# Hybrid decoder block on one core: first four row tiles transposed by TensorE, other buffer counts, sub-norm factors folded into the output weights

## The chip, the cores and the metric

The kernel runs on one core of one Trainium2 chip. The metric is the device time of one execution in microseconds, the median of several runs. The engines are TensorE (PE; PEld is its weight load), VectorE (DVE), ScalarE (ACT), GpSimd (POOL) and SyncE (SP), which issues nearly all DMAs.

## The reference

One layer on x of 2048 tokens by 1024 features, f32:

```
h    = RMSNorm(x)
cq, ckv, kr, dq, dk, dv, mq, z = split(h @ w_in)      # D_IN = 2464
A    = latent attention, 8 heads: causal softmax(q k^T / sqrt(96)) v, q and k normed, 32 of 96 columns rotated
B    = differential attention, 4 heads: (softmax_1 - lambda softmax_2) v, then
       rms_norm(o, diff_subln_g) * (1 - lam_init)      # the sub-norm, per head of 64 columns
C    = cross attention of the tokens into 256 memory tokens (4 heads), memory normed and projected first
out  = x + (concat(A, B, C) * silu(z)) @ w_out         # 512 + 256 + 256 columns
```

## The kernel before, in words

Tokens lie in 16 row tiles of 128, and four of these make a block (b = 0 to 3). Every f32 operand of a projection is split into a high and a low f16 half, and a product is three matmuls, high by high, high by low, low by high (`project`, lines 173 to 178).

`normed_t` (lines 129 to 140) takes one row tile: ScalarE squares and sums it (L132), GpSimd makes the reciprocal root (`rstd_of`, L97 and L101), ScalarE writes the scaled tile rounded to f16, the high half (L134), VectorE writes the remainder, the low half (L138). Both halves need features on the partitions, so SP issues one DMA transpose for each (L136, L139) into `ht`, 128 x 2 x 8 x 128. These DMA instructions are collected in the list `turned`. `load` (lines 116 to 122), which fetches rows and weights, looks at this list: as long as it has between 1 and 11 entries, the load is issued under `tc.issue_after` an entry some places back (3 or 6). That adds an order, without a semaphore, behind the named instruction for those instructions of the block that are on its engine. So SP issues the early loads behind transposes.

`m_prep` for block 0 (lines 1049 to 1074) fetches rows 0 to 3 and the first weights and norms the four tiles; then `x_feed` does the other twelve tiles, and `mem_kv` norms the memory's two tiles in the same way and projects them. `rope_tables` (lines 252 to 289) makes the rotary tables from the positions, in two scratch tiles of the tag `t4`, which has two buffers.

The work goes in 28 steps: 4 of C ("m"), 8 of B ("d", two head pairs by four blocks), 16 of A ("a", four head pairs by four blocks). A step has a preparation (projection, norms, rotation, transposes, estimate of the row maximum) and a main part.

- The estimate is `est_block` (lines 374 to 408). It computes the scores of high halves alone. For blocks 1 to 3 ScalarE copies the first score tile of a row tile into `er` as bf16 (L391), each further one into `ec` (L394), and VectorE takes the larger of `er` and `ec` (L395). Two row tiles share one `er`; after both, VectorE halves it three times (L399) and reduces it (L400). There are 96 such pairs in the kernel. `er` has two buffers, `ec` three. The maximum goes into the query operand as a further row, so the main scores come out shifted by it.
- The main part is `Map` (lines 475 to 524). `head` computes a score tile on TensorE (`st`), ScalarE writes its exponential as f32 into `p32` (L493; the profile calls this tile p), VectorE writes the low part into `plo` (L494). `tail` multiplies the upper 16 bits of `p32` (L503, L505) and `plo` (L523) with the values. `p32` has three buffers, `plo` four, the score tile two of PSUM.
- After a d step `post_d` (lines 577 to 594) applies the sub-norm: squares on ScalarE, the reciprocal root on GpSimd, then three VectorE passes over 128 x 512: by the root (L588), by the gain `g_sub` that holds (1 - lam_init) / 64 (L589), by the gate (L592).

`load_wout` (lines 920 to 929) fetches the output weights in chunks of 128 rows and splits them, scaled by WS = 64; chunks 4 and 5 are those of B. `out_tile` divides by it again with a factor 0.5 / WS.

What sets the order: preparations, main units and fills (`fills`, lines 1146 to 1160: memory, further rows, gates, latents, output projection) are generators. A loop (lines 1189 to 1225) advances the one with the least due time, worked out from costs written by hand. That gives the order in which instructions are traced, and with offsets a priority. From these a scheduler, which keeps a simulated time line, writes each engine's fixed order. A tile with n buffers makes the writer of use i wait for the readers of use i - n.

Of the kernel before, what the change touches and what calls it, by code (L numbers as in the profile page):

```python
# [11 lines left out]
F32 = mybir.dt.float32  # L12
F16 = mybir.dt.float16
BF16 = mybir.dt.bfloat16
# [5 lines left out]
P = 128  # L20
# [20 lines left out]
def hybrid_block(ctx: ExitStack, tc: tile.TileContext, x, mem, positions, norm_g, w_in, mla_q_norm_g,  # L41
# [84 lines left out]
        load(xt, src, pace)  # L126
        return xt

    def normed_t(xt, name):
        hi = stack([P, DM], f"xh_{name}")  # L130
        ss = sm.tile([P, 1], F32, tag="ss1", name=f"ss_{name}")
        A.activation(hi, xt, AF.Square, scale=1.0 / math.sqrt(DM), accum_out=ss)  # L132
        r = rstd_of(ss, [1], f"r_{name}", "rstd_x")
        A.activation(hi, xt, AF.Copy, scale=r)  # L134
        ht = bigt([P, 2, NK, P], f"ht_{name}")
        turned.append(SP.dma_start_transpose(ht[:, 0], hi))  # L136
        lo = stack([P, DM], f"xl_{name}")
        V.scalar_tensor_tensor(lo, xt, r, hi, ALU.mult, ALU.subtract)  # L138
        turned.append(SP.dma_start_transpose(ht[:, 1], lo))  # L139
        return ht  # L140


# [48 lines left out]
    def tmp4(name):  # L191
        return wk.tile([P, 1024], F32, tag="t4", name=name, bufs=2)
# [57 lines left out]
    sin_t = cst.tile([P, NT, 16], F32, name="sin_t")  # L250

    def rope_tables():
        pos_i = wk.tile([P, NT], I32, tag="posi", name="pos_i")
        SP.dma_start(pos_i, positions[0].rearrange("(t p) -> p t", p=P))
        pos_f = wk.tile([P, NT], F32, tag="posf", name="pos_f")
        V.tensor_copy(pos_f, pos_i)
        inv = np.float32(10000.0) ** (-np.arange(0, 32, 2, dtype=np.float32) / np.float32(32))
        inv_t = wk.tile([P, 16], F32, tag="invt", name="inv_t")
        for i in range(16):
            G.memset(inv_t[:, i:i + 1], float(inv[i]))  # L260
        w1 = tmp4("rp1")
        w2 = tmp4("rp2")
        ang = w1[:, 0:256]
        k = w1[:, 256:512]
        h = w1[:, 512:768]
        r = w1[:, 768:1024]
        a3 = ang.rearrange("p (t f) -> p t f", f=16)
        V.tensor_tensor(a3, _bc(pos_f, 2, 16), _bc(inv_t, 1, NT), ALU.mult)
        magic = 12582912.0
        V.tensor_scalar(k, ang, 1.0 / math.pi, magic, ALU.mult, ALU.add)  # L270
        V.tensor_scalar_sub(k, k, magic)
        p1 = 201.0 / 64.0
        p2 = math.pi - p1
        e2 = 2.0 ** (math.floor(math.log2(p2)) - 10)
        p2 = math.floor(p2 / e2) * e2
        p3 = math.pi - p1 - p2
        V.scalar_tensor_tensor(r, k, -p1, ang, ALU.mult, ALU.add)
        V.scalar_tensor_tensor(r, k, -p2, r, ALU.mult, ALU.add)
        V.scalar_tensor_tensor(r, k, -p3, r, ALU.mult, ALU.add)
        V.tensor_scalar(h, k, 0.5, -0.25, ALU.mult, ALU.add)  # L280
        V.tensor_scalar_add(h, h, magic)
        V.tensor_scalar_sub(h, h, magic)
        V.scalar_tensor_tensor(h, h, -2.0, k, ALU.mult, ALU.add)
        V.tensor_scalar(h, h, -2.0, 1.0, ALU.mult, ALU.add)
        V.scalar_tensor_tensor(w2[:, 0:256], r, -1.0, r, ALU.mult, ALU.max)
        A.activation(w2[:, 256:512], r, AF.Sin)
        A.activation(w2[:, 512:768], w2[:, 0:256], AF.Sin, scale=-1.0, bias=halfpi)
        V.tensor_tensor(sin_t.rearrange("p t f -> p (t f)"), w2[:, 256:512], h, ALU.mult)
        V.tensor_tensor(cos_t.rearrange("p t f -> p (t f)"), w2[:, 512:768], h, ALU.mult)
# [4 lines left out]
    g_k = gain_row(mla_kn_g, 96, "g_k")  # L294
    g_n = cst.tile([P, 64], F32, name="g_n")
    V.tensor_tensor(g_n, g_q[:, 0:64], g_k[:, 0:64], ALU.mult)
    g_sub = gain_row(diff_subln_g, 64, "g_sub")
    V.tensor_scalar_mul(g_sub, g_sub, (1.0 - LAM_INIT) / WS)
    lamw = tmp4("lamw")
    lamt = lamw[:, 0:128].rearrange("p (a b) -> p a b", b=32)  # L300
    SP.dma_start(lamt.rearrange("p a b -> p (a b)"), diff_lambda.rearrange("o a b -> o (a b)").broadcast_to([P, 128]))
# [72 lines left out]
    def est_block(st, i, nmap, mcol, lhs, rhs):  # L374
# [3 lines left out]
        for m in range(nmap):  # L378
            for t in range(4):
                if fold and t % 2 == 0:  # L380
                    er = wk.tile([P, 2, 512], BF16, tag="er", name="er", bufs=2)
                for c in range(b + 1):
                    ps = ps_e.tile([P, 512], F32, tag="pe", name="pe")
                    n = (4 if c < b else t + 1) * P
# [5 lines left out]
                    elif c == 0:  # L390
                        A.activation(er[:, t % 2], ps, AF.Copy)  # L391
                    else:
                        ec = wk.tile([P, 512], BF16, tag="ec", name="ec", bufs=3)
                        A.activation(ec[:, 0:n], ps[:, 0:n], AF.Copy)  # L394
                        V.tensor_tensor(er[:, t % 2, 0:n], er[:, t % 2, 0:n], ec[:, 0:n], ALU.max)  # L395
                    yield 0.5
# [78 lines left out]
    class Map:  # L475
# [9 lines left out]
        def head(self, j):  # L485
# [1 line left out]
            n = (4 - t0) * P  # L487
            ps = ps_s.tile([P, 512], F32, tag="st", name="st")
            self.scores(ps, j, t0, n, j >= self.diag0)
            p32 = wk.tile([P, 512], F32, tag="p32", name="p32", bufs=3)  # L490
            plo = wk.tile([P, 512], F16, tag="plo", name="plo", bufs=4)
            phi = p32.bitcast(BF16).rearrange("p (n t) -> p n t", t=2)[:, :, 1]
            A.activation(p32[:, :n], ps[:, :n], AF.Exp, scale=self.scale)  # L493
# [83 lines left out]
    def post_d(st, y):  # L577
# [5 lines left out]
            A.activation(sink[:, 64 * i:64 * i + 64], y8[:, i, :], AF.Square, scale=1.0 / 8.0, accum_out=ss[:, i:i + 1])  # L583
        yield 1.0
        r = rstd_of(ss[:, 0:8], [8], f"yr_{st.name}", "rstd_y")
        yield 1.0
        yield 1.0
        V.tensor_tensor(y8, y8, _bc(r, 2, 64), ALU.mult)  # L588
        V.tensor_tensor(y8, y8, _bc(g_sub, 1, 8), ALU.mult)  # L589
        yield 1.0  # L590
        yf = y.rearrange("p t h d -> p t (h d)")
        V.tensor_tensor(yf, yf, st.z, ALU.mult)  # L592
# [327 lines left out]
    def load_wout(cs):  # L920
        for c in cs:
# [1 line left out]
            SP.dma_start(f, w_out[0, c * P:(c + 1) * P, :])  # L923
            yield 1.0
            wt = bigt([P, 2, 1024], f"wo{c}")
            A.activation(wt[:, 0, :], f, AF.Copy, scale=WS)
            V.scalar_tensor_tensor(wt[:, 1, :], f, WS, wt[:, 0, :], ALU.mult, ALU.subtract)
            wout[c] = wt
            yield 1.0

# [116 lines left out]
    def m_prep(st):  # L1047
        b = st.b
        if b == 0:
# [1 line left out]
                xts.append(fetch_rows(x[0, P * i:P * i + P, :], f"x{i}", big))  # L1051

            def norm(i):
                hts.append(normed_t(xts[i], f"x{i}"))

            xts = []
            row(0)
# [191 lines left out]
```

## Time and profile before

| | us |
|---|---|
| median of 3 runs | 1398.42 (1397.34 to 1401.3) |
| the profiled execution | 1403.92 |
| its span | 1402.0 |
| TensorE matmul busy | 1303.8 (93%) |
| VectorE busy | 1111.0 (79%) |
| ScalarE busy | 898.9 (64%) |
| GpSimd busy | 352.1 (25%) |

The span is the time between the first and last recorded instruction. Matmuls are pipelined and their ends are modelled, so TensorE's busy time is not work at its peak rate; two matmuls in a row can overlap in the record. A bracket at the end of a row tells how long the engine had been idle and what released it. The mean granted clock of TensorE was 0.978 of full.

### The profile page before, as it was taken

The numbers are of one execution on the slowest core, as the hardware profiler recorded it, in microseconds if no ns is written. First come the engines' busy times: TensorE is split into PE (matmuls) and PEld (weight loads), VectorE is DVE, ScalarE is ACT, GpSimd is POOL, SyncE is SP. The second block draws the span as 40 slices with busy tenths as digits, with TensorE's granted clock in tenths as the row PEclk, the third lists the DMA queues.
The fourth block names the chain that finished last, engine by engine and source line by source line (L and its number), as shares of the span: only waits on it lengthen the run. The fifth ranks groups of instructions, "written<-read, shape, count | busy, mean of one in ns | idle before, by whom it ended". The sixth has DMA issues, their size and how long they took to land.

```text
span 1402.0 us, 35085 instructions
## 1 busy us (share of the span) xinstructions
PE 1303.8 (93%) x13552; PEld 830.8 (59%) x13552; DVE 1111.0 (79%) x2649; ACT 898.9 (64%) x2153; POOL 352.1 (25%) x541
## 2 busy tenths in 40 slices
PE   4789899999989999998998899999998898999998
PEld 1344456667678666666675656656655665655554
DVE  3458787989799858887897888978898899975645
ACT  5646443778786747775885767756776797763521
POOL 2222133304043033104113143353333503200000
PEclk9999999999999999999999999999999999999999
DMA  8999764144133123347255266535545353265462
GB/s 206 247 218 198 163 121 98 39 81 80 43 54 77 40 39 61 74 118 186 93 103 140 42 148 144 123 86 148 122 95 111 83 107 68 48 117 177 116 214 71
DMA packets 302695, 157.66 MB, mean 112 GB/s; under 512 B 248384, under 2 KB 281280, under 8 KB 302528
## 3 DMA queue, kind: packets, MB, share of 16 engines
q1 hardware_dynamic: 302496, 155.42, 48.7%
q8 instruction: 106, 1.74, 0.5%
q14 instruction: 61, 0.50, 0.1%
q0 software_dynamic: 32, 0.00, 0.0%
HBM read 61.79 MB, written 34.34 MB: 69 GB/s over the span
## 4 chain that ended last, share of the span: by engine, by line
PE 59%; DVE 13%; DMA 10%; POOL 6%; ACT 5%; issue 4%; SPq 2%; ACTq 0%; DVEq 0%; POOLq 0%
PE pp L176 6%; PE pp L177 6%; PE pp L178 6%; PE pe L385 6%; PE pv L505 4%; PE pv L503 3%; DVE plo L494 3%; PE pv L523 3%; PE pp L943 3%; PE pp L945 3%; PE pp L944 3%; DMA qB_a<-qs_a 3%; PE st L559 3%; PE st L903 3%; PE st L904 2%
## 5 line engine op out<-in xcount | busy, mean ns | idle before, releaser
L493 ACT ACTIVATE p<-st 128x512 f32<-128x512 f32 (+3 forms) x672 | 356.3, 548 | 210.3 <-PE st L905 81.4
L494 DVE TENSOR_TENSOR plo<-p 128x512 f16<-128x512 f32 (+3 forms) x672 | 406.3, 618 | 70.3 <-ACT p L493 67.8
L394 ACT ACTIVATE ec<-pe 128x512 bf16<-128x512 f32 (+3 forms) x384 | 196.1, 538 | 29.5 <-PE pe L387 11.7
L503 PEld LDWEIGHTS <-p 128*128 128x128 bf16 x2304 | 185.6, 100 | 48.6 <-DVE y_d L566 7.4
L505 PEld LDWEIGHTS <-p 128*128 128x128 bf16 x2304 | 172.3, 98 | 39.9 <-issue 2.9
L395 DVE TENSOR_TENSOR er<-er,ec 128x512 bf16<-128x512 bf16 (+3 forms) x384 | 143.0, 375 | 28.7 <-ACT ec L394 24.1
L523 PEld LDWEIGHTS <-plo 128*128 128x128 f16 x2304 | 120.8, 98 | 24.6 <-DVE plo L494 12.8
L391 ACT ACTIVATE er<-pe 128x512 bf16<-128x512 f32 x192 | 118.0, 617 | 24.0 <-PE pe L385 20.7
L176 PEld LDWEIGHTS <-ht_x 128*128 128x128 f16 x896 | 88.6, 99 | 72.2 <-DMA ht_x<-xh_x 20.9
L903 PE MATMUL st<-qB_a,kT_a 97*128 97x512 f16 (+1 forms) x320 | 113.4, 354 | 11.2 <-ACT p L493 10.2
L178 PEld LDWEIGHTS <-ht_x 128*128 128x128 f16 x896 | 88.7, 99 | 55.6 <-DMA ht_x<-xl_x 4.9
L177 PEld LDWEIGHTS <-ht_x 128*128 128x128 f16 x896 | 88.7, 99 | 54.2 <-issue 7.5
L503 PE MATMUL pv<-V_d,p 128*128 128x65 f16 x1088 | 115.8, 194 | 5.3 <-DVE y_d L566 3.9
L559 PE MATMUL st<-qB_d,kT_d 97*128 97x512 f16 (+1 forms) x320 | 112.0, 353 | 5.4 <-ACT p L493 4.7
L505 PE MATMUL pv<-V_d,p 128*128 128x64 f16 x1088 | 115.8, 196 | 0.0
L904 PE MATMUL st<-qB_a,kT_a 96*128 96x512 f16 (+1 forms) x320 | 112.9, 353 | 0.0
L905 PE MATMUL st<-qB_a,kT_a 96*128 96x512 f16 (+1 forms) x320 | 111.9, 350 | 0.0
L503 PE MATMUL pv<-V_a,p 128*128 128x65 f16 x1088 | 111.0, 193 | 0.0
L505 PE MATMUL pv<-V_a,p 128*128 128x64 f16 x1088 | 110.8, 195 | 0.0
L385 PE MATMUL pe<-kT_d,qB_d 96*128 96x512 f16 (+2 forms) x320 | 102.9, 350 | 5.8 <-DMA qB_d<-s_d 2.8
L385 PE MATMUL pe<-kT_a,qB_a 96*128 96x512 f16 (+2 forms) x320 | 93.6, 349 | 12.4 <-DMA qB_a<-qs_a 8.6
L176 PE MATMUL pp<-w_d,ht_x 128*128 128x512 f16 x256 | 97.0, 379 | 0.3 <-ACT ql L185 0.3
(285 smaller groups left out, 3335.2 us busy)
## 6 DMA issues: line engine op xcount, KB each, us to landing
xt_x<-in_x_dram SPq DMA_DIRECT2D x16, 512.0 KB, 4.8
xr<-in_x_dram SPq DMA_DIRECT2D x16, 512.0 KB, 3.8
part<-xr SPq DMA_DIRECT2D x16, 512.0 KB, 2.9
ysc<-yt SPq DMA_DIRECT2D x31, 256.0 KB, 2.0
yl<-ysc SPq DMA_DIRECT2D x15, 512.0 KB, 4.3
zsc<-zc SPq DMA_DIRECT2D x48, 128.0 KB, 2.3
xa<-part SPq DMA_DIRECT2D x12, 512.0 KB, 3.8
out_dram<-xa SPq DMA_DIRECT2D x12, 512.0 KB, 3.2
```

The source lines that it names most:

```text
L176: T.matmul(ps[:, :n], lhsT=ht[:, 0, k], rhs=wt[:, 0, :n], start=(k == 0), stop=False)
L177: T.matmul(ps[:, :n], lhsT=ht[:, 0, k], rhs=wt[:, 1, :n], start=False, stop=False)
L178: T.matmul(ps[:, :n], lhsT=ht[:, 1, k], rhs=wt[:, 0, :n], start=False, stop=(k == NK - 1))
L385: T.matmul(ps[:, 0:n], lhsT=lhs(m, t), rhs=rhs(m, c, n // P), start=True, stop=c < b)
L394: A.activation(ec[:, 0:n], ps[:, 0:n], AF.Copy)
L493: A.activation(p32[:, :n], ps[:, :n], AF.Exp, scale=self.scale)
L494: V.tensor_tensor(plo[:, :n], p32[:, :n], phi[:, :n], ALU.subtract)
L503: T.matmul(pvv[:, t, 0:65], lhsT=phi[:, c], rhs=vt[:, 0:65], start=(j == 0 and t == 0), stop=False, skip_group_check=True)
L505: T.matmul(pvv[:, t, 0:64], lhsT=phi[:, c], rhs=vt[:, 65:129], start=False, stop=False, skip_group_check=True)
L523: last["pv"] = T.matmul(pvv[:, t, 0:65], lhsT=plo[:, c], rhs=vt[:, 0:65], start=False, stop=(j == self.njt - 1), skip_group_check=True)
L559: T.matmul(ps[:, :n], lhsT=st.kTs[j // 4][0:97, h, j % 4, m % 2, :], rhs=st.qB[h][0:97, t0:4, m % 2, :], start=True, stop=not diag)
L903: T.matmul(ps[:, :n], lhsT=kt[0:97, h, j % 4, 0, :], rhs=q[0:97, 0, t0:4, :], start=True, stop=False)
```

## The change

There are five edits.

1. `normed_t` gets a flag, set for the first four row tiles alone. With it each half is transposed by a new function, `turn`: eight matmuls with the half's 128 x 128 pieces as the stationary operand and the identity as the moving one, four into each of two PSUM tiles (the pool of the estimate's scores), then two copies to SBUF as f16, the first by ScalarE, the second by VectorE. `turned` gets that last copy.
2. The maximum tile `er` has one buffer instead of two, the copy tile `ec` four instead of three.
3. The f32 tile `p32` has four buffers instead of three.
4. The gain of the sub-norm moves into the output weights: chunks 4 and 5 are scaled by a column `g_wo` (the gain, twice over the 128 rows, by (1 - lam_init) WS) instead of WS; `post_d` loses the pass with `g_sub` and scales the reciprocal root by 1 / WS on GpSimd.
5. The positions and the frequencies of the rotary tables lie in the second scratch tile instead of in tiles of their own.

```diff
--- before.py
+++ after.py
@@ -126,17 +126,28 @@
         load(xt, src, pace)
         return xt
 
-    def normed_t(xt, name):
+    def turn(dst, src):
+
+        for h in range(2):
+            ps = ps_e.tile([P, 512], F32, tag="pe", name="pt")
+            for k in range(4):
+                T.matmul(ps[:, k * P:k * P + P], lhsT=src[:, (4 * h + k) * P:(4 * h + k + 1) * P], rhs=ident,
+                         start=(k == 0), stop=(k == 3), skip_group_check=True)
+            d = dst[:, 4 * h:4 * h + 4].rearrange("p k c -> p (k c)")
+            last = V.tensor_copy(d, ps) if h else A.activation(d, ps, AF.Copy)
+        return last
+
+    def normed_t(xt, name, on_pe=False):
         hi = stack([P, DM], f"xh_{name}")
         ss = sm.tile([P, 1], F32, tag="ss1", name=f"ss_{name}")
         A.activation(hi, xt, AF.Square, scale=1.0 / math.sqrt(DM), accum_out=ss)
         r = rstd_of(ss, [1], f"r_{name}", "rstd_x")
         A.activation(hi, xt, AF.Copy, scale=r)
         ht = bigt([P, 2, NK, P], f"ht_{name}")
-        turned.append(SP.dma_start_transpose(ht[:, 0], hi))
+        turned.append(turn(ht[:, 0], hi) if on_pe else SP.dma_start_transpose(ht[:, 0], hi))
         lo = stack([P, DM], f"xl_{name}")
         V.scalar_tensor_tensor(lo, xt, r, hi, ALU.mult, ALU.subtract)
-        turned.append(SP.dma_start_transpose(ht[:, 1], lo))
+        turned.append(turn(ht[:, 1], lo) if on_pe else SP.dma_start_transpose(ht[:, 1], lo))
         return ht
 
 
@@ -250,16 +261,16 @@
     sin_t = cst.tile([P, NT, 16], F32, name="sin_t")
 
     def rope_tables():
-        pos_i = wk.tile([P, NT], I32, tag="posi", name="pos_i")
+        w1 = tmp4("rp1")
+        w2 = tmp4("rp2")
+        pos_i = w2[:, 768:784].bitcast(I32)
         SP.dma_start(pos_i, positions[0].rearrange("(t p) -> p t", p=P))
-        pos_f = wk.tile([P, NT], F32, tag="posf", name="pos_f")
+        pos_f = w2[:, 784:800]
         V.tensor_copy(pos_f, pos_i)
         inv = np.float32(10000.0) ** (-np.arange(0, 32, 2, dtype=np.float32) / np.float32(32))
-        inv_t = wk.tile([P, 16], F32, tag="invt", name="inv_t")
+        inv_t = w2[:, 800:816]
         for i in range(16):
             G.memset(inv_t[:, i:i + 1], float(inv[i]))
-        w1 = tmp4("rp1")
-        w2 = tmp4("rp2")
         ang = w1[:, 0:256]
         k = w1[:, 256:512]
         h = w1[:, 512:768]
@@ -294,8 +305,10 @@
     g_k = gain_row(mla_kn_g, 96, "g_k")
     g_n = cst.tile([P, 64], F32, name="g_n")
     V.tensor_tensor(g_n, g_q[:, 0:64], g_k[:, 0:64], ALU.mult)
-    g_sub = gain_row(diff_subln_g, 64, "g_sub")
-    V.tensor_scalar_mul(g_sub, g_sub, (1.0 - LAM_INIT) / WS)
+    g_wo = cst.tile([P, 1], F32, name="g_wo")
+    for i in range(2):
+        SP.dma_start(g_wo[64 * i:64 * i + 64, :], diff_subln_g[0].rearrange("(p o) -> p o", o=1))
+    V.tensor_scalar_mul(g_wo, g_wo, (1.0 - LAM_INIT) * WS)
     lamw = tmp4("lamw")
     lamt = lamw[:, 0:128].rearrange("p (a b) -> p a b", b=32)
     SP.dma_start(lamt.rearrange("p a b -> p (a b)"), diff_lambda.rearrange("o a b -> o (a b)").broadcast_to([P, 128]))
@@ -378,7 +391,7 @@
         for m in range(nmap):
             for t in range(4):
                 if fold and t % 2 == 0:
-                    er = wk.tile([P, 2, 512], BF16, tag="er", name="er", bufs=2)
+                    er = wk.tile([P, 2, 512], BF16, tag="er", name="er", bufs=1)
                 for c in range(b + 1):
                     ps = ps_e.tile([P, 512], F32, tag="pe", name="pe")
                     n = (4 if c < b else t + 1) * P
@@ -390,7 +403,7 @@
                     elif c == 0:
                         A.activation(er[:, t % 2], ps, AF.Copy)
                     else:
-                        ec = wk.tile([P, 512], BF16, tag="ec", name="ec", bufs=3)
+                        ec = wk.tile([P, 512], BF16, tag="ec", name="ec", bufs=4)
                         A.activation(ec[:, 0:n], ps[:, 0:n], AF.Copy)
                         V.tensor_tensor(er[:, t % 2, 0:n], er[:, t % 2, 0:n], ec[:, 0:n], ALU.max)
                     yield 0.5
@@ -487,7 +500,7 @@
             n = (4 - t0) * P
             ps = ps_s.tile([P, 512], F32, tag="st", name="st")
             self.scores(ps, j, t0, n, j >= self.diag0)
-            p32 = wk.tile([P, 512], F32, tag="p32", name="p32", bufs=3)
+            p32 = wk.tile([P, 512], F32, tag="p32", name="p32", bufs=4)
             plo = wk.tile([P, 512], F16, tag="plo", name="plo", bufs=4)
             phi = p32.bitcast(BF16).rearrange("p (n t) -> p n t", t=2)[:, :, 1]
             A.activation(p32[:, :n], ps[:, :n], AF.Exp, scale=self.scale)
@@ -583,10 +596,10 @@
             A.activation(sink[:, 64 * i:64 * i + 64], y8[:, i, :], AF.Square, scale=1.0 / 8.0, accum_out=ss[:, i:i + 1])
         yield 1.0
         r = rstd_of(ss[:, 0:8], [8], f"yr_{st.name}", "rstd_y")
+        G.tensor_scalar(r, r, 1.0 / WS, None, ALU.mult)
         yield 1.0
         yield 1.0
         V.tensor_tensor(y8, y8, _bc(r, 2, 64), ALU.mult)
-        V.tensor_tensor(y8, y8, _bc(g_sub, 1, 8), ALU.mult)
         yield 1.0
         yf = y.rearrange("p t h d -> p t (h d)")
         V.tensor_tensor(yf, yf, st.z, ALU.mult)
@@ -923,8 +936,9 @@
             SP.dma_start(f, w_out[0, c * P:(c + 1) * P, :])
             yield 1.0
             wt = bigt([P, 2, 1024], f"wo{c}")
-            A.activation(wt[:, 0, :], f, AF.Copy, scale=WS)
-            V.scalar_tensor_tensor(wt[:, 1, :], f, WS, wt[:, 0, :], ALU.mult, ALU.subtract)
+            s = g_wo if c in (4, 5) else WS
+            A.activation(wt[:, 0, :], f, AF.Copy, scale=s)
+            V.scalar_tensor_tensor(wt[:, 1, :], f, s, wt[:, 0, :], ALU.mult, ALU.subtract)
             wout[c] = wt
             yield 1.0
 
@@ -1051,7 +1065,7 @@
                 xts.append(fetch_rows(x[0, P * i:P * i + P, :], f"x{i}", big))
 
             def norm(i):
-                hts.append(normed_t(xts[i], f"x{i}"))
+                hts.append(normed_t(xts[i], f"x{i}", True))
 
             xts = []
             row(0)
```

## Rows read from the trace of the kernel before

**Rows 1.** Stages: window, length, PE, PEld, DVE, ACT, POOL busy (count), clock, DMA share, GB/s.
```profile
0.00:40.00 40.00, 20.46 (x72) 7.64 (x72) 15.67 (x29) 20.71 (x33) 7.53 (x40) 0.96 0.87 216
40.00:60.00 20.00, 11.50 (x40) 4.04 (x40) 11.11 (x14) 11.60 (x19) 6.69 (x8) 0.83 1.11 269
60.00:160.00 100.00, 92.50 (x533) 45.06 (x532) 65.23 (x115) 54.96 (x96) 23.00 (x41) 0.95 0.95 194
160.00:300.00 140.00, 139.58 (x1262) 84.41 (x1261) 115.85 (x308) 77.58 (x210) 40.23 (x53) 1.00 0.46 95
300.00:1402.00 1102.00, 1039.72 (x11652) 689.60 (x11650) 903.14 (x2186) 734.07 (x1799) 274.61 (x399) 0.98 0.43 101
```

**Rows 2.** Time line of TensorE at the start: start, duration, instruction, idle and releaser.
```profile
16.15 0.61 PE L176 MATMUL pp<-w_m,ht_x 128*128 128x512 f16 x1 [16.15 <-DMA ht_x<-xh_x]
...
24.33 0.38 PE L176 MATMUL pp<-w_m,ht_x 128*128 128x512 f16 x1 [2.64 <-ACT w_m L168]
...
43.96 0.39 PE L178 MATMUL pp<-w_m,ht_x 128*128 128x512 f16 x1 [3.09 <-DMA ht_x<-xl_x]
```

**Rows 3.** Time line of the same stretch: norms, transposes and loads.
```profile
7.60 1.15 ACT L134 ACTIVATE xh_x<-xt_x,r_x 128x1024 f16<-128x1024 f32 x1 [1.02 <-POOL r_x L101]
...
12.07 1.34 SPq L136 DMA_TRANSPOSE ht_x<-xh_x  x1
...
31.22 1.28 DVE L138 SCALAR_TENSOR_TENSOR xl_x<-xt_x,r_x,xh_x 128x1024 f16<-128x1024 f32 x1 [2.75 <-ACT xh_x L134]
...
37.16 2.19 SPq L139 DMA_TRANSPOSE ht_x<-xl_x  x1
...
41.60 1.06 ACT L132 ACTIVATE xh_m<-xt_m 128x1024 f16<-128x1024 f32 x1 [1.03 <-DMA xt_m<-in_mem_dram]
```

**Rows 4.** Nearest operations: identity matmul, its successor's start, copies out of PSUM.
```profile
1378.46 0.22 PE L907 MATMUL st<-mask_t,ident 128*128 128x128 bf16 x1
1378.52 0.19 PE L503 MATMUL pv<-V_a,p 128*128 128x65 f16 x1
...
L391 ACT ACTIVATE er<-pe x192: 572/605/764, 242.0 to 1310.0; 128x512 bf16<-128x512 f32 x192
...
L647 DVE TENSOR_REDUCE mx_m<-pe x32: 676/681/693, 85.2 to 187.1; 128x2 f32<-128x512 f32 x32
```

**Rows 5.** A short stretch in which SP issued mostly transposes; columns as Rows 1.
```profile
75.00:80.00 5.00, 5.00 (x24) 2.25 (x23) 1.81 (x2) 3.19 (x6) 0.79 (x2) 1.00 1.07 221
```

**Rows 6.** Who waited for whom: us in total, times, longest.
```profile
PE st L903 <- ACT p L493: 10.2, 14, 1.6
PE pv L523 <- DVE plo L494: 8.7, 8, 2.3
...
ACT p L493 <- PE st L905: 81.4, 67, 6.6
...
ACT p L493 <- PE pv L505: 26.2, 21, 4.9
```

**Rows 7.** Time line of `er`: next pair's first copy and last pair's reduction.
```profile
245.26 0.59 ACT L391 ACTIVATE er<-pe 128x512 bf16<-128x512 f32 x1
...
247.11 0.29 DVE L400 TENSOR_REDUCE mx_d<-er 128x2 f32<-128x128 bf16 x1
...
1307.00 0.60 ACT L391 ACTIVATE er<-pe 128x512 bf16<-128x512 f32 x1 [0.24 <-PE pe L385]
...
1309.40 0.28 DVE L400 TENSOR_REDUCE mx_a<-er 128x2 f32<-128x128 bf16 x1
```

**Rows 8.** The sub-norm's pass and GpSimd's scaling, by line: ns min/median/max.
```profile
L589 DVE TENSOR_TENSOR y_d<-y_d,g_sub x8: 678/682/802, 276.9 to 817.0; 128x512 f32<-128x512 f32 x8
...
L97 POOL TENSOR_SCALAR yr_d<-yss_d x8: 243/415/2357, 269.8 to 812.0; 128x8 f32<-128x8 f32 x8
```

**Rows 9.** Time line of VectorE: the tables' last write and first use.
```profile
116.41 0.42 DVE L289 TENSOR_TENSOR cos_t<-rp,rp 128x256 f32<-128x256 f32 x1
...
189.13 0.42 DVE L341 TENSOR_TENSOR sq_d<-qkv_d,rt_d 128x256 f32<-128x256 f32 x1
```

## The prediction, made before the changed kernel was run

> **What bounds the kernel now.** I read the table by stages first, then TensorE's waits, then the start in order of time, then the waits of the long middle. The stages [rows 1] differ: TensorE is busy 20.5 of the first 40 us, 11.5 of the next 20, 92.5 of the 100 after that, 139.6 of 140 up to 300 us, and 1039.7 of the remaining 1102. So of 98 us without a matmul, 28.0 lie in the first 60 us, 7.5 in the next 100, and 62.3 are scattered over the last 1102. From 160 us on, the DMA engines are under half busy; before, they are at 0.87, 1.11 and 0.95 of their sum: the start is fed by DMA, the rest is a TensorE-bound body with gaps. The reader is to see in TensorE's rows [rows 2] what ends the early gaps: the first matmul stands at 16.15 us, released by the transposed high half of the first row tile; 2.64 us go on the weights; 3.09 us on the low half of the fourth tile, at 43.96. The granted clock is 0.83 of full in 40 to 60 us, where TensorE had stood idle [rows 1]: a gap also costs some half-speed time behind it. At 60 us TensorE has work queued in every stage, so what the first 60 us finish earlier, the end can see.
>
> **The change part by part.**
>
> *Four tiles turned by TensorE.* Eight DMA transposes go (two halves of four tiles). Each moves 128 x 1024 x 2 bytes = 0.262 MB, together 2.1 MB. On the path: the first high half is ready when its ACTIVATE ends, 7.60 + 1.15 = 8.75 us, its transpose is issued at 12.07 and the matmul starts at 16.15: 7.4 us [rows 2, 3]. For the fourth tile the low half is ready at 31.22 + 1.28 = 32.50, issued at 37.16, used at 43.96: 11.5 us [rows 2, 3]. In their place each half takes 8 matmuls of 128 columns and two copies out of PSUM, one on ScalarE, one on VectorE. Nearest rows [rows 4]: the matmul against the identity lasts 0.22 us and the next one starts 0.06 us behind it; a ScalarE copy of 128x512 out of PSUM takes 0.605, a VectorE pass over as much PSUM 0.681. So a half is ready about 4 x 0.06 + 0.22 + 0.68 = 1.1 us after its source, 2 us with waits between engines: 11.5 - 2 = 9.5 us are saved on the fourth tile, 5.4 on the first. TensorE's 64 added matmuls take 64 x 0.06 = 4 us, at half clock 8; they lie inside the 28 us that are idle. ScalarE gets 8 x 0.605 = 4.8 us and VectorE 8 x 0.681 = 5.4; in the first 40 us these are busy 20.7 and 15.7 us, so there is room. If that cover were gone, the copies would give back those 5 us.
>
> In DMA time: the stage up to 40 us moves 216 GB/s, a stretch that carries mostly transposes 221 [rows 1, 5]; 2.1 MB at that rate is 9.7 us of a resource that is full. Path and resource agree on about 9.5 us. The Trainium skill (Advanced Engine Details and Errata, X-Bar Transpose) says that transposing DMAs are as fast as others, 350 to 400 GB/s. By that the eight would hold the engines 2.1 MB / 375 GB/s = 5.6 us (an estimate from the page), and the part's gain would be 5.6 us. This stretch's row has 221 GB/s at a share of 1.07, so the trace does not agree.
>
> *The pace of loads.* `load` orders each early DMA behind a transpose in SP's queue, by an edge on the engine of the instruction named in `turned`. For the first eight entries that instruction is now a VectorE copy, so an edge on its engine holds no SP load: the third and fourth weight unit, rows 2 and 3 and the memory rows (whose first use waits until 41.60) may be issued without the transposes ahead [rows 3]. The 2.64 us wait for weights can go [rows 2]; I take 2.5. Below nothing is possible too, as early memory loads compete with the weights: bounds -5 to +3. What is late next is ScalarE: norms, weights and copies before the first block's last projection.
>
> Start together: -9.5 - 2.5 = -12. Bounds: -16 (28.0 us idle, less the 9 until a first half can exist and 3 for the weights) and -2 (the 60 to 160 us stage, DMA-bound at 0.95, takes the rest back).
>
> *A fourth f32 tile and copy tile.* ScalarE waited 26.2 us, 21 times, for pv matmuls that still read the f32 tile; TensorE in turn waited 10.2 for ScalarE's exponentials and 8.7 for VectorE's low parts [rows 6]. Upper end 18.9 us, lower end 0, or 3 lost if scores run ahead of more urgent work. ScalarE's waits for scores are larger, 81.4 us [rows 6]: TensorE is what is late, mostly. I take -4, a fifth of the upper end, nearer to nothing.
>
> *One maximum tile.* With two tiles the next pair's first ScalarE copy may start before the last pair's reduction. Subtracting the starts of those copies from the ends of the reductions over all pairs: in 78 of 95 handovers it does, by 345.5 us in all, 4.4 each; the first by 247.40 - 245.26 = 2.1 us, the last by 1309.68 - 1307.00 = 2.7 [rows 7]. With one tile the copy waits, and behind it on ScalarE the exponentials of the main chain, for which TensorE waits. From the nearest rows: 26.2 us of ScalarE waits went with 10.2 of TensorE, 0.39 of it [rows 6]. If each of 78 handovers made ScalarE wait a whole fold (three maxima and a reduction, at 0.28 us each by the reduction's row, 1.1 us), that is 86 us and 34 on TensorE; lower end 0, if other ScalarE work is ordered into the gap. The estimates are made well ahead of their use, so I take +4 (0.13 us of ScalarE per handover), nearer to the lower end.
>
> *The norm factor folded.* Eight VectorE passes go, 8 x 0.682 = 5.5 us; eight POOL scalings of 8 columns come, median 0.415 each [rows 8], in the same chain in front of VectorE. The scale of the weights turns from a constant to a column in the same instructions; one small DMA is added. VectorE is not what ends (903 of 1102 us busy against 1040 [rows 1]): I take 0, bounds -5 and +2.
>
> *Rope tables.* The positions' load now waits for a scratch tile, and SP stands behind it. The tables were ready at 116.83 us and first used at 189.13 [rows 9]: 72 us cover a delay. 0; without cover, what a shared scratch tile is late, some 10 us; SP's queue held up meanwhile could cost 3.
>
> Sum: -12 - 4 + 4 = -12. The profiled execution took 1403.92 us (span 1402.0 and 1.9 around it), so 1391.9; the median of the runs is 1398.42, 5.5 below, so **1386.4**.
>
> **The rivals.**
>
> *The start's gain is taken back.* The other 24 transposes of rows stay on DMA, the 60 to 160 us stage is at 0.95 of the engines with only 7.5 us of TensorE idle; if its pace is set by those tiles, only 2 us survive: 1398.4 - 2 = 1396.4. Against it: that stage loses the 9.7 us of DMA work ahead of it and starts earlier. The skill's rule above lies on this side, at 1398.4 - 5.6 = 1392.8; the 221 GB/s row speaks against it, and its chance of 0.05 is in this rival's.
>
> *The single maximum tile costs more than the start gives (slower).* Place: the first copy of each pair on ScalarE. It decides from the point where its cost passes 16 us, that is 16 / 0.39 / 78 = 0.53 us of ScalarE wait per handover. At 0.8 us it is 78 x 0.8 x 0.39 = 24: 1398.4 - 12 - 4 + 24 = 1406.4. For it: VectorE is busy 82% of the body, and a fold queues behind its other work; against it: the order of instructions is made knowing the single tile.
>
> *The buffers pay in full.* The 18.9 us of TensorE waits go, and the single tile costs 4: 1398.4 - 12 - 18.9 + 4 = 1371.5. For it: those waits lie in the body where nothing else ends them; against it: ScalarE waits three times longer for scores than for tiles.
>
> *The change does not do what it says* can't well be: the transposes are named instructions. That they move but the first matmul stays at 16 us, for lack of weights, is in the first rival.
>
> **How the numbers follow.** Forecast 0.50 (1380 to 1393 by itself), start taken back 0.15, single tile 0.18, buffers in full 0.17. What a measurement can tell from no change is about 0.3%, 4.2 us. Faster: forecast 0.50, buffers 0.17 and the skill's part 0.02: 0.69; same 0.14; slower 0.17. The range takes most of the rivals on both sides, 1371 to 1406.
>
> **What would show it.** Right: no DMA transposes of the first four tiles, a first projection matmul near 11 us instead of 16.15, the memory rows' norm near 30 instead of 41.60, the idle time of 0 to 60 us down from 28 to about 16, and d-stage events all some 12 us earlier; ScalarE's 26.2 us wait for pv down to a few. Wrong: equal TensorE idle at 160 us, or idle beyond 300 us well above 62, with ScalarE's copies into the maximum tile ended by VectorE's reduction; the forecast fails as a whole if that wait is over 0.5 us a pair.

## The result, and the profile after

The changed kernel took 1385.23 us (median of 8 runs, 1378.37 to 1389.19) and the kernel before, on the same chip, 1397.93 (8 runs, 1393.63 to 1404.07). The ratio is 0.9898, 95% interval 0.9876 to 0.992. The forecast was 1386.4, so time and sign came out as forecast. The terms of its sum did not: in the experiments below the start is worth about 4 us instead of 12, the three buffer counts together 9 instead of 0, the fold costs 6 us on one kernel and gives 7 on another, and some 7 us belong to no edit by itself.

Busy time by stage of the changed kernel, columns as in [rows 1]:

```profile
0.00:40.00 40.00, 23.26 (x138) 11.79 (x138) 22.63 (x40) 27.35 (x45) 7.68 (x24) 1.00 0.75 233
40.00:60.00 20.00, 17.68 (x81) 7.75 (x82) 10.73 (x14) 13.17 (x24) 8.16 (x14) 1.00 0.87 189
60.00:160.00 100.00, 89.70 (x540) 43.63 (x539) 69.38 (x124) 58.54 (x102) 26.41 (x55) 0.97 0.92 191
160.00:300.00 140.00, 138.32 (x1243) 83.47 (x1242) 115.77 (x310) 77.57 (x212) 39.61 (x50) 1.00 0.42 89
300.00:1380.70 1080.70, 1028.61 (x11624) 687.80 (x11620) 895.14 (x2166) 726.14 (x1784) 271.57 (x406) 0.98 0.43 103
```

TensorE's idle time in the first 60 us fell from 28.0 to 60 - 23.26 - 17.68 = 19.1 us. From 60 to 160 us it rose from 7.5 to 10.3, and after 300 us it fell from 62.3 to 1080.7 - 1028.6 = 52.1. So of the 8.9 us that the first 60 us gained, about 4 were lost again by 300 us, and the body gained 10.2.

TensorE's time line at the start (start, duration, instruction, idle and releaser), which answers to [rows 2]:

```profile
9.00 1.03 PE L134 MATMUL pt<-ident,xh_x 128*128 128x128 bf16 x8 [9.00 <-ACT xh_x L145]
10.31 1.03 PE L134 MATMUL pt<-ident,xl_x 128*128 128x128 bf16 x8 [0.28 <-DVE xl_x L149]
11.14 0.63 PE L187 MATMUL pp<-w_m,ht_x 128*128 128x512 f16 x1
...
32.66 0.38 PE L134 MATMUL pt<-ident,xl_x 128*128 128x128 bf16 x4 [3.24 <-DVE ht_x L137]
41.21 0.39 PE L189 MATMUL pp<-w_m,ht_x 128*128 128x512 f16 x1 [1.67 <-ACT ht_x L137]
```

The first tile went as the prediction had it: eight matmuls turn a half in 1.03 us, and the first projection starts at 11.14 instead of 16.15. The last tile did not: its low half is used at 41.21 instead of 43.96. At 32.66 TensorE itself had stood 3.24 us until VectorE copied an earlier turned piece out of PSUM; the pool has three tiles. ScalarE and SP show why, in the same view (answers to [rows 3]):

```profile
34.62 5.01 ACT L179 ACTIVATE w_mkv<-wst_mkv,gm 128x512 f16<-128x512 f32 x8
39.52 1.06 ACT L143 ACTIVATE xh_m<-xt_m 128x1024 f16<-128x1024 f32 x1
40.47 0.20 ACT L143 ACTIVATION_READ_ACCUMULATOR xh_m<-xt_m 128x1 f32 x1
40.56 0.59 ACT L137 ACTIVATE ht_x<-pt 128x512 f16<-128x512 f32 x1
```

```profile
29.57 3.71 SPq L619 DMA_DIRECT2D zsc<-zc  x2
33.33 0.91 SPq L120 DMA_DIRECT2D xt_m<-in_mem_dram  x2
```

The ScalarE copy of that half stands behind eight conversions of the memory's weights (5.01 us) and a norm. The memory rows' load was no longer ordered behind transposes, but in SP's fixed order it stands behind the stores of the gates, which SP began at 29.57 us and which held it for 3.71; the memory's norm starts at 39.52 (41.60 before), not near 30. The d stage starts earlier too, but by less than the 12 us of the forecast: its first score by 8.7 us (214.4 instead of 223.1).

**The positions' load.** The fifth edit reaches the start as well. Before, SP issued the positions' load at 4.47 us, the entry behind it held SP until 10.05, and the first transposes came behind that [rows 3]. In the changed kernel this load needs the scratch tile and goes out at 94.78. Below are SP's rows before, SP's row in the changed kernel, and TensorE's rows in e2, the kernel with every edit but the first:

```profile
4.47 0.43 SPq L254 DMA_DIRECT2D pos_i<-in_positions_dram  x1
4.95 5.10 SPq L85 DMA_DIRECT2D g_mk<-in_mem_kn_g_dram  x1
...
94.78 0.58 SPq L267 DMA_DIRECT2D rp<-in_positions_dram  x1
...
13.85 0.61 PE L176 MATMUL pp<-w_m,ht_x 128*128 128x512 f16 x1 [13.85 <-DMA ht_x<-xh_x]
...
39.50 0.39 PE L178 MATMUL pp<-w_m,ht_x 128*128 128x512 f16 x1 [0.93 <-DMA ht_x<-xl_x]
```

In each of the seven kernels that keep the load in the first 20 us, the entry behind it lasts 3.96 to 5.89 us. With the load late and every transpose still on DMA, e2 starts its first projection at 13.85 us and uses the fourth tile's low half at 39.50, earlier than the changed kernel's 41.21 (e6: 14.71 and 40.56). So the 2.75 us that the fourth tile gained can't be put down to TensorE's transposes.

**A measure for where the time goes.** Every kernel here does the same TensorE work, if the matmuls that turn tiles are left out: the moving columns of all matmul rows, divided by 2.4 GHz, are 1201.7 us in each trace. Summing those of the matmuls that started before a given time tells how far ahead of the kernel before a kernel is. Lead in us of work, from one profile each:

```
at us          60    160    300    500    700    1000   1200
after          9.4    6.4    4.6    4.4   13.4   20.0   16.5
e1 edit 1      3.2    4.7    4.9    5.0    6.9   11.0    7.4
e2 rest        4.9    2.1   -1.6   -2.9    6.6    5.9    3.8
e3 free loads  3.4    3.6    3.4    5.5   10.2   10.6    8.7
e4 one max     0.6    0.6    0.5   -4.9    0.0    0.2   -9.0
e5 buffers     0.4    1.4   -3.1   -1.7    5.4   11.5    9.7
e6 max, p32    4.1    0.9   -0.4   -1.2    4.7    2.9    3.7
e7 fold        0.2   -0.2   -0.6   -2.3    0.3   10.1    0.9
e8 rest, free  5.8    0.9   -1.4    0.8   10.3   18.7   15.8
e9 lead only   0.6   -0.2   -1.8    0.0    5.5    9.9    6.8
e10 no fold    8.3    6.2    5.8   -3.7    3.3   15.1   10.1
e11 eight      5.5    5.8    3.4    3.7   11.1   17.3   14.6
e12 DVE copies 7.7    3.4   -0.1    5.5   14.6   25.3   23.9
```

The profiled execution before was 5.5 us over the median of its runs, and most kernels gain on it between 500 and 700 us, the control e9 too; so the columns from 700 on are to be compared among the kernels. The start's lead in the changed kernel is 9.4 us at 60 and 4.6 at 300. The kernels e2, e6 and e8 move the positions' load and turn nothing on TensorE; they lead by 4.1 to 5.8 us at 60 and by 0.9 to 2.1 at 160. The kernels e4, e5 and e7, which leave that load early, have 0.2 to 0.6 at 60. So about half of the 9.4 us goes with the fifth edit, and in e2, e6 and e8 most of that is gone by 160.

**The granted clock.** TensorE's busy time differs between kernels that do the same work (e12 has the 64 turning matmuls besides): 1303.8 us before, 1307.2 in e4, 1295.0 in e5, 1290.2 in e12, at a mean granted clock of 0.978, 0.974, 0.980 and 0.990 of full. It goes with the time of one kernel's runs too: a straight line through the 24 runs of the kernel before that stand beside e5 to e8 falls by 8.6 us for each 0.01 of granted clock. Part of a difference between kernels can thus be a difference of the clock. Whether the clock made the time shorter, or fewer gaps let the clock stay high, is not shown.

### The profile page after: what moved, and what is told of

It is laid out like the page before. It is cut to its first block, busy times and chain, and to the rows that moved or that the text cites. A ratio compares the mean times of both kernels' runs of the same rounds, so it can differ in the third digit from the quotient of the medians.

```text
span 1380.7 us, 35076 instructions
## 1 busy us (share of the span) xinstructions
PE 1297.6 (94%) x13616; PEld 834.4 (60%) x13616; DVE 1113.6 (81%) x2649; ACT 902.8 (65%) x2163; POOL 353.4 (26%) x549
## 4 chain that ended last, share of the span: by engine, by line
PE 53%; DVE 14%; DMA 10%; POOL 9%; ACT 8%; issue 5%; SPq 1%; ACTq 0%; POOLq 0%; DVEq 0%
PE pp L187 6%; PE pp L188 6%; PE pp L189 6%; PE pe L398 5%; DVE plo L507 4%; PE pv L518 3%; PE pv L516 3%; PE pv L536 3%; PE st L572 3%; PE pp L957 3%; PE pp L958 3%; PE pp L959 3%; POOL r_a L101 2%; PE st L916 2%; PE st L917 2%
## 5 line engine op out<-in xcount | busy, mean ns | idle before, releaser
L404 ACT ACTIVATE er<-pe 128x512 bf16<-128x512 f32 x192 | 110.2, 606 | 44.2 <-DVE mx_d L413 14.1
L536 PEld LDWEIGHTS <-plo 128*128 128x128 f16 x2304 | 123.6, 98 | 24.0 <-DVE plo L507 8.6
L916 PE MATMUL st<-qB_a,kT_a 97*128 97x512 f16 (+1 forms) x320 | 112.6, 352 | 19.2 <-ACT p L506 14.3
L516 PE MATMUL pv<-V_a,p 128*128 128x65 f16 x1088 | 113.9, 194 | 0.4 <-DVE y_a L923 0.4
L398 PE MATMUL pe<-kT_d,qB_d 96*128 96x512 f16 (+2 forms) x320 | 106.4, 351 | 6.0 <-ACT ec L407 3.5
L398 PE MATMUL pe<-kT_a,qB_a 96*128 96x512 f16 (+2 forms) x320 | 102.4, 353 | 6.6 <-DMA qB_a<-qs_a 3.1
```

Of the source, the lines that this page charges most:

```text
L398: T.matmul(ps[:, 0:n], lhsT=lhs(m, t), rhs=rhs(m, c, n // P), start=True, stop=c < b)
L516: T.matmul(pvv[:, t, 0:65], lhsT=phi[:, c], rhs=vt[:, 0:65], start=(j == 0 and t == 0), stop=False, skip_group_check=True)
L536: last["pv"] = T.matmul(pvv[:, t, 0:65], lhsT=plo[:, c], rhs=vt[:, 0:65], start=False, stop=(j == self.njt - 1), skip_group_check=True)
```

## The experiments

Each has its median, and the ratio to the kernel before on the same chip with its 95% interval. Lines left out of a diff repeat the changed kernel's, and a diff with several counts in one line is a short form. The scheduler writes a new order for every kernel, so each difference also holds what the new order did; e9 gives a size for that.

### e1: the first edit alone

```diff
-                hts.append(normed_t(xts[i], f"x{i}"))
+                hts.append(normed_t(xts[i], f"x{i}", True))
```

> Only the first edit: the first four row tiles transposed by TensorE, all buffers, the sub-norm and the rope scratch as before. Theory (the start gives it, the other edits cancel): 12 us faster than the kernel before, ratio 0.991; TensorE idle of the first 60 us down from 28 to about 19, the first score exponential of the first d step about 8 us earlier, ScalarE's wait for pv matmuls that hold the f32 tile still about 26 us. Rival (the start's gain is taken back by the DMA-bound stretch, the buffers pay): within 3 us of before, ratio 0.998 to 1.0.

1394.19 us, ratio 0.9969 (0.9952 to 0.9986): 4.3 us faster. In its profile the lead stays near 5 us from 160 to 500, and TensorE's idle time of the first 60 us is 19.9 us, as expected. The gain is clear of noise, but about a third of what the sum had for the start, and hardly more than a new order alone gave in e9.

### e2: all edits but the first

```diff
-er bufs=2   ec bufs=3   p32 bufs=3
+er bufs=1   ec bufs=4   p32 bufs=4     (and the sub-norm fold, the rope scratch)
```

> Everything but the first edit: DMA transposes as before, one maximum tile, four copy and f32 tiles, sub-norm factor in the weights, rope scratch. Theory: nothing, within 4 us of before, ratio 0.997 to 1.003, with ScalarE waiting some 10 to 30 us on the maximum's reduction and 10 to 15 less on the f32 tile. Rival (the buffers and the lighter VectorE pay): 12 us faster, ratio 0.991, and then the first experiment shows little.

1397.98 us, ratio 0.9988 (0.9969 to 1.0006): nothing to tell from no change, as the theory had it. ScalarE's waits came nearly as foreseen as well: 31.7 us for the reduction, and 10.6 instead of 26.2 for the pv matmuls that hold the f32 tile. So 15.6 us less of that wait went with no gain in time. But e1 and e2 together give 6 us, and the changed kernel has 14 by its ratio.

### e3: the loads freed, transposes still on DMA

```diff
-        if 0 < len(turned) < 2 * NPACE:
+        if False:
```

> The kernel before with one thing taken away: loads are no longer ordered behind transposes, which stay on DMA. It tells how much of the start's gain is the loads' freedom. Theory: 2.5 us faster by the weights' wait that goes (ratio 0.998), as the transposes still take some 9.5 us on the path. Rival 1 (freed loads are the gain): 12 us faster, ratio 0.991. Rival 2 (the order was needed): slower by 3 us or more, since row and weight loads take the DMA engines from the transposes.

1394.26 us, ratio 0.9974 (0.9951 to 0.9997): 3.6 us faster, within noise the whole of what the first edit gave, with all transposes on DMA. What e1 measured can thus be the loads' freedom for the most part, a side of the edit that the prediction had at 2.5 of 12.

### e4: one maximum tile alone

```diff
-er = wk.tile([P, 2, 512], BF16, tag="er", name="er", bufs=2)
+er = wk.tile([P, 2, 512], BF16, tag="er", name="er", bufs=1)
```

> The kernel before with one maximum tile instead of two, nothing else. Theory: 4 us slower (ratio 1.003), ScalarE waiting about 0.13 to 0.4 us per handover for the reduction, 10 to 30 us in all. Rival (the single tile is what the start's gain pays for): 24 us slower, ratio 1.017, with 0.8 us per handover. Second rival: no cost at all, as other ScalarE work is ordered into the gap.

1416.87 us, ratio 1.0125 (1.0098 to 1.0152): 17.5 us slower, four times the term. Who waited for whom in e4 (us in total, times, longest):

```profile
ACT er L391 <- DVE mx_d L400: 17.4, 14, 2.3
...
ACT er L391 <- DVE mx_a L400: 10.1, 9, 4.8
...
PE st L903 <- ACT p L493: 10.1, 12, 3.1
...
PE pv L523 <- DVE plo L494: 10.0, 9, 4.1
...
PE pe L385 <- ACT ec L394: 8.6, 8, 3.0
```

ScalarE waits 27.5 us for the reduction: 0.35 for each of the 78 handovers that overlapped before, instead of 0.13. At the prediction's price of 0.39 that would be 10.7 us. TensorE's own waits for ScalarE's copies rose only from 4.3 to 8.6; the rest of the 17.5 us is not in a single wait.

### e5 and e6: the buffer counts

e5 is the kernel before with the three counts; e6 leaves the copy tile at three and takes the rope scratch for room.

```diff
 e5: er bufs=1, ec bufs=4, p32 bufs=4
 e6: er bufs=1, ec bufs=3, p32 bufs=4, rope tables' inputs in w2
```

> The kernel before with the three buffer counts alone (one maximum tile, four copy tiles, four f32 tiles). The single maximum tile cost 17.5 us alone, all edits but the first -1.7, so 19 us are given by the copy tile, the f32 tile and the sub-norm. Theory A (the f32 tile gives it, by ScalarE's waits for pv that fall from 26 to about 11 us): this kernel equals before within 4 us, ratio 0.998 to 1.003. Theory B (the lighter sub-norm on VectorE gives it): this one stays about 15 us slower, ratio 1.011. Theory C (orders of instructions differ from kernel to kernel by several us, whatever the edit): anything between.

> The kernel before with one maximum tile and four f32 tiles; the copy tile stays at three, the sub-norm as before, and the rope tables lie in the scratch tile to make room. It splits the f32 tile from the copy tile. Theory A (f32 tile): within 4 us of the kernel with all three counts. Rival (the copy tile lets ScalarE go on past the maximum tile's wait): some 10 us slower than before.

e5: 1390.28 us, ratio 0.9938 (0.9914 to 0.9961), 8.7 us faster than before. e6: 1399.92, ratio 1.0014 (0.9992 to 1.0035), nothing to tell from before. So from e4 on, 17.5 - 2.0 = 15.5 us go with the fourth f32 tile (and the moved rope tables), and 10.7 more with the fourth copy tile (and the tables back in their place).

None of the named theories held as written. Theory A had e5 within 4 us of before because ScalarE's waits for pv would fall to about 11 us; e5 is 8.7 us faster, and these waits are 22.0 us in it, as in e4 (22.5). They are down to 14.5 in e6, whose time is that of before within noise. And e6 lies 10.7 us behind e5, not within 4; the rival had such a size, but against the kernel before. In e5, same view as for e4:

```profile
ACT p L493 <- PE pv L505: 22.0, 15, 3.2
...
ACT er L391 <- DVE mx_a L400: 16.3, 15, 3.2
...
ACT er L391 <- DVE mx_d L400: 14.6, 15, 2.1
...
PE st L903 <- ACT p L493: 6.2, 11, 2.2
...
PE pe L385 <- ACT ec L394: 4.1, 7, 1.1
...
PE pv L523 <- DVE plo L494: 3.4, 8, 1.0
```

The reader is to see that ScalarE waits for the single maximum tile as long as in e4 (30.9 us against 27.5), while TensorE's waits are down from e4: for exponentials from 10.1 to 6.2, for low parts from 10.0 to 3.4, for copies from 8.6 to 4.1, 15.0 us in all. That fits a wait which is not removed but covered by tiles made earlier. It does not prove it. Of the 23.9 us between the spans of the two profiles, 12.2 are TensorE's busy time for the same work, at the granted clocks given above. And in the changed kernel, with the same three counts, these waits of TensorE are not down:

```profile
PE st L916 <- ACT p L506: 14.3, 14, 4.3
ACT er L404 <- DVE mx_d L413: 14.1, 12, 2.9
...
ACT er L404 <- DVE mx_a L413: 13.0, 14, 2.9
...
ACT p L506 <- PE pv L518: 11.5, 12, 3.8
...
PE pe L398 <- ACT ec L407: 6.3, 9, 1.9
...
PE pv L536 <- DVE plo L507: 5.6, 6, 1.9
```

TensorE's three make 26.2 us, against 23.2 before (10.2, 8.7 and 4.3). So the runs show what the counts do to the time, and not by which wait.

### e7: the sub-norm factor alone

```diff
-        V.tensor_tensor(y8, y8, _bc(g_sub, 1, 8), ALU.mult)
+        G.tensor_scalar(r, r, 1.0 / WS, None, ALU.mult)
```

> The kernel before with the sub-norm's gain folded into the output weights, nothing else. 5.5 us of VectorE go, which is 80% busy beside a TensorE that is 93% busy. Theory: within 4 us of before, ratio 0.997 to 1.003. Rival (VectorE ends what TensorE waits for in the d stage): up to 6 us faster, more if the shorter chain after a step lets the next step's tiles go earlier.

1402.98 us, ratio 1.0042 (1.0022 to 1.0062): 5.9 us slower, outside the bounds of the term (-5 to +2), with 5.5 us less work for VectorE. Neither the theory nor the rival held.

### e8: the changed kernel without TensorE's transposes, loads free

```diff
 all edits but the first, and
-        if 0 < len(turned) < 2 * NPACE:
+        if False:
```

> All edits but the first, and the loads freed of their order behind transposes, which stay on DMA: the changed kernel without TensorE's transposes, but with the freedom that they bring the loads. Freed loads alone gave 3.6 us, the first edit alone 4.4. Theory (the loads' freedom is what the first edit gives): as fast as the changed kernel, ratio 0.990 of before, within 4 us of it. Rival (the transposes taken off DMA count once the buffers are there): stays at about 0.997, some 9 us slower than the changed kernel.

1383.09 us, ratio 0.9894 (0.9872 to 0.9915): as fast as the changed kernel, without one matmul that turns a tile. But the gain does not come through the start. The stages of e8:

```profile
0.00:60.00 60.00, 34.38 (x138) 13.53 (x139) 26.93 (x42) 33.65 (x55) 14.68 (x32) 0.97 0.87 233
60.00:160.00 100.00, 87.62 (x508) 42.13 (x507) 64.53 (x114) 58.40 (x100) 24.68 (x57) 0.97 0.95 194
160.00:300.00 140.00, 137.87 (x1258) 83.82 (x1257) 116.32 (x304) 74.83 (x201) 39.52 (x54) 1.00 0.45 95
300.00:1000.00 700.00, 675.80 (x7902) 470.05 (x7899) 605.68 (x1520) 507.42 (x1291) 199.60 (x289) 0.99 0.44 98
```

Up to 300 us it has started 138 + 508 + 1258 = 1904 matmuls, the kernel before 1906 (111 + 533 of the first 160 us in the same view, and 1262 in [rows 1]), the changed one 1938 without the 64. So of the 5.8 us that e8 leads by at 60 us nothing is left at 300. It makes its gain between 300 and 1000 us: 7902 matmuls there, against 7629 before and 7869 in the changed kernel. The start's freedom, which changes nothing of the body's instructions, is worth 3.6 us on the kernel before and 13.1 on e2. The granted clock of e8's runs is on average 0.008 above that of the runs before on its chip, that of e2's 0.005: at 8.6 us for each 0.01 some 3 of the 13.1 us go with the clock (an estimate).

### e9: a control, another order

```diff
-    LEAD = 11.0
+    LEAD = 11.25
```

> A control: the kernel before with one scheduling number changed, the lead of preparations from 11.0 to 11.25 of the hand-written cost units. No instruction is added or taken away and no buffer changes; only the written order differs. Theory C (an order that differs moves the time by several us, whatever the edit): 3 to 8 us away from before in either direction, with TensorE's work equal up to 160 us and apart after 300. Rival (the time follows the edits alone): within 2 us, ratio 0.9985 to 1.0015.

1393.85 us, ratio 0.9978 (0.996 to 0.9996): 3.1 us faster by the ratio, 3.9 by the medians. One number that adds no instruction and no buffer moved the time about as much as the first edit did. The interval is near to 1, so it is shown that order matters, not by how much in general.

### e10: the changed kernel without the fold

```diff
-        G.tensor_scalar(r, r, 1.0 / WS, None, ALU.mult)
+        V.tensor_tensor(y8, y8, _bc(g_sub, 1, 8), ALU.mult)
```

> The changed kernel without its fourth edit, so the sub-norm's pass with the gain is back on VectorE. The fold alone cost 5.9 us on the kernel before. Theory (the fold's cost is its own, by the longer chain through POOL): about 6 us faster than the changed kernel, ratio 0.986 of before. Rival (its cost was that of another order): within 4 us of the changed kernel on either side, or slower by what VectorE gets back, 5.

1388.97 us, ratio 0.9947 (0.9927 to 0.9967): slower than the changed kernel by 0.49% of before, 6.9 us (3.7 by the medians, which come from two chips). The same edit costs 5.9 on one kernel and gives 6.9 on the other. The theory of a cost of its own fell, and the rival, slower by about 5, came near. What the edit does to the time by itself can't be told from what the new order does.

### e11: eight tiles by TensorE

```diff
-            hts.append(normed_t(xt, f"x{i}"))
+            hts.append(normed_t(xt, f"x{i}", i < 8))
```

> The changed kernel with eight row tiles instead of four transposed by TensorE. In the changed kernel TensorE was 9.4 us of work ahead of before at 60 us, and 4.5 at 100. Theory (the DMA-bound stretch of 60 to 160 us takes half of the lead back): with eight transposes less in that stretch, some 10 us of DMA time, the lead at 160 us grows from 6 to 9 or more, and the time falls by 3 to 5 us, ratio 0.987. Rival (ScalarE and VectorE, who make the copies, set the pace by then): lead and time unchanged or worse.

1387.1 us, ratio 0.9927 (0.99 to 0.9953): no gain over the changed kernel. The lead at 160 us is 5.8, not 9. But it was only 5.5 at 60 us, so between 60 and 160 us nothing of it was lost, where the changed kernel lost 3.0. By the time the rival held; that DMA-bound transposes take the lead back in that stretch is neither shown nor excluded, as the start differs by 3.9 us as well.

### e12: both copies on VectorE

```diff
-            last = V.tensor_copy(d, ps) if h else A.activation(d, ps, AF.Copy)
+            last = V.tensor_copy(d, ps)
```

> The changed kernel with both copies of a turned half on VectorE instead of one on ScalarE. In the changed kernel the fourth tile's low half was used only at 41.21 us (43.96 before), its ScalarE copy queued behind eight weight conversions of 5 us. Theory (ScalarE's queue ate the fourth tile's gain, and what is late behind it is the DMA-bound stretch): the fourth tile's last matmul starts 3 to 5 us earlier, TensorE is some 12 us of work ahead of before at 60 us instead of 9.4, but the lead at 160 us stays 5 to 8, and the time stays within 4 us of the changed kernel, ratio 0.987 to 0.993. Rival (the start's lead lasts): the lead grows at 160 and 300 us too, and the time falls by 3 us or more.

1380.77 us, ratio 0.9864 (0.983 to 0.9898), the fastest of all; against the changed kernel the two intervals overlap. Its fourth tile's low half is used at 39.69, only 1.5 us earlier; its lead is 7.7 at 60 us and gone at 300. Its stages:

```profile
160.00:300.00 140.00, 136.04 (x1249) 82.71 (x1247) 113.45 (x300) 74.89 (x205) 38.27 (x53) 1.00 0.45 90
300.00:1000.00 700.00, 679.23 (x7970) 472.53 (x7969) 612.92 (x1535) 516.63 (x1308) 193.40 (x290) 1.00 0.43 99
```

The theory's mechanism fell, and so did the rival's. What it won, it won in the body again, with 7970 matmuls in the 700 us and a granted clock of 1.00. These rows flatter it: the profile is of its fastest run, 1372.23 us, 8.5 below its median.

## Why the prediction was right or wrong, point by point

- **What bounds the kernel.** Right in the two stages; wrong in the step "what the first 60 us finish earlier, the end can see". Of 9.4 us at 60 us, 4.6 are left at 300; e12 is the fastest with none left.
- **Four tiles on TensorE, -9.5.** The operations cost what their nearest rows said: identity matmul 0.22 us, ScalarE copy 0.596 median, VectorE copy 0.684 [rows 4]. The term was mis-sized in the step from there to "9.5 us are saved on the fourth tile": that tile gained 2.75 us, and e2, without TensorE's transposes, gained 4.46 at the same place. "There is room" on ScalarE was a share, while the copy stood in a fixed order behind 5 us of other work. The path that the term counted as the transposes' also held the positions' load, which stood in SP's queue ahead of the first of them. That path and DMA time "agree" had no bearing on the time: e11 took eight more transposes off DMA and gained no time. The row with 221 GB/s was misread, too: in the trace, 0.52 of the 1.1 MB that began in it moved in packets of 4096 bytes (rows of x) and 0.45 in packets of 256 bytes (the transposes). So it is no rate of transposes. Of the first 40 us the trace has a price, beside other traffic: 1.94 MB in packets of 256 bytes took 198 us of the 16 engines' time, 12.4 us of all 16, so the 9.7 us of DMA time were if anything low. The start, loads included, gave 4.3 us (e1) where the sum had 12. The rival "the start's gain is taken back" came nearer to that size.
- **The pace of loads, -2.5.** Right that the edge vanishes. It gives 3.6 us by itself (e3); with e1 at 4.3 the two can't be told apart by time.
- **f32 and copy tile, -4.** Mis-sized: 26 us, counted from e4 to e5, more than the "upper end" of 18.9, so TensorE's waits for exponentials and low parts were no bound. ScalarE's waits for pv fell from 26.2 to 11.5 us (12 times) in the changed kernel, not to "a few"; by e2 and e5 the time does not follow them.
- **One maximum tile, +4.** Mis-sized: 17.5 alone (e4), though below the bound of 34. Both factors were low: ScalarE waits 0.35 us a handover instead of 0.13, and a microsecond of that wait goes with 0.64 us of time (17.5 of 27.5) instead of 0.39. So the cost passed 16 us at 0.35 us, not at 0.53. Alone it was the slower rival, and it is more than the start's 4.3. With the other two counts, the three give -8.7, where the sum had 0.
- **The fold, 0.** Its total in the sum can't be called right: +5.9 alone, -6.9 inside.
- **Rope tables, 0.** Right in what it looked at: the tables are last written at 125.68 us instead of 116.83 and first used at 182.68. It missed that moving the positions' load frees SP in the first 10 us, the opposite of "SP's queue held up", with 4 to 6 us of lead at 60 us in e2, e6 and e8. No run has this edit alone, so what it is worth in the end stays open.

The sum of the parts alone is -4.3 - 8.7 + 5.9 = -7.1 us, the ratio of the whole -14.3, that of e2 -1.7 and of e8 -14.8. So some 7 us belong to no edit by itself; with the intervals of the four ratios that is 7 give or take 6. It can go the other way: e1 and e5 give 13 us together, and e10, which has both of them and the rope edit, 7.4. That the order of instructions, which every edit changes all over the body, moves the time is shown by e9 at 3 to 4 us, and e7 against e10 agree with it. That it accounts for all of the 7 us, or for the 13.1 us of e8 over e2, is not shown: I have no run that holds the body's order fixed while the start changes, and which pieces of the order matter is left open. That the forecast of the time was met to 1.2 us was luck: 8 us too much for the start, 9 too little for the buffers, 6 that the fold costs alone and 7 that no part accounts for nearly cancelled.

## What to carry to other kernels

When buffers are traded (one tile fewer here, one more there), run both sides apart and as a pair: ScalarE's wait for the scarce tile was about 30 us in a kernel that was 17.5 us slower than before and in one that was 8.7 us faster. The size of one wait did not give the time. Look also at what stands behind a small load in a DMA queue: the entry behind the positions' load held SP for about 5 us, and half of the lead at 60 us goes with moving that load. An engine that is half busy still makes a copy late if its order is fixed: look at what stands ahead of the instruction, not at the share. Where a scheduler writes the order anew for every edit, make a control that changes nothing but the order; here it moved the time 0.2%, and the same edit came out at +5.9 and at -6.9 us on two kernels, so parts of this size can't be added up.
